# A hybrid encoder block on one core: one pool for value stage and pairs, sums on VectorE, weights loaded earlier, values of two heads computed in the attention stage

## The chip, the cores and the metric

The kernel runs on one core of a Trainium2 chip. A core has a matrix engine (TensorE, PE in the profile, with its weight loads as PEld), VectorE (DVE), ScalarE (ACT), GpSimd (POOL) and SyncE (SP), which issues DMAs. Compute engines read and write tiles in the on-chip memory; matmuls write into eight banks of accumulators. The metric is the device time of one execution in microseconds; the median of several runs is compared.

## The reference, cut to what matters

```
h  = rmsnorm(x) * (1 + scale) + shift               # scale, shift, gate from silu(c) @ w_ada
q, k, v, z_gla, ra_f, ra_b, u, vs, z_gmlp, m_gla, m_gmlp = split(h @ w_in)
# branch 1: 4 heads of gated linear attention in both directions, chunks of 64 tokens;
# decays from ra_f, ra_b; q, k of 128 columns a head, v of 256 columns a head
o     = rmsnorm(o_forward + o_backward) * gla_norm_g
y_gla = (o * silu(z_gla)) @ w_br_gla
# branch 2: spatial gating in chunks of 128 tokens
sg     = einsum(gmlp_ws, layernorm(gelu(vs))) + gmlp_bs
y_gmlp = (gelu(u) * sg * silu(z_gmlp)) @ w_br_gmlp
out = rmsnorm(x + gate * ((sigmoid(m_gla) * y_gla + sigmoid(m_gmlp) * y_gmlp) @ w_out)) * final_g
```

All is 1024 tokens by 1024 columns in float32.

## The kernel before, in words

Every large matmul works on operands split in two: a rounded part ("hi", cast on ScalarE) and the rest ("lo", subtracted on VectorE); `split_w` makes both, and three matmuls (hi·hi, hi·lo, lo·hi) stand for one product over 128 rows. The stages, in program order:

1. **Norm and vs, first half.** `h` (the activation `H`, 16 tiles of two chunks by 512 tokens, hi and lo) is made while the first half of vs is computed.
2. **Layer norm and spatial mixing** (`vs1`, `ln`, `spatial`). The power of the norm runs on GpSimd. The mixed rows `sg` go to DRAM.
3. **Value stage.** `dense_v23` (heads 2 and 3, 512 columns at once), `dense_v0` (head 0 with the 32 gate logits `ra`, 288 columns) and `dense_v1` (head 1). Each token tile's values are split by `v_out` and stored to DRAM on SP's queue. Beside it `sums` makes sums and differences of four quarters of H (the tiles `TS`, t0 to t3): four additions and four subtractions per call on GpSimd (L459 to L468), then four splits.
4. **Pairs** (`pair`, 16 of them). Two blocks of 128 output columns are computed together from the sums (a scheme that needs seven products instead of eight). Two raw weight tiles `wa`, `wb`, their sums `wsum` (four half-size additions on GpSimd, L574 to L581), and four splits per pair. The evaluation gives u, z_gmlp and the two merge gates, which go to DRAM. Half of the second-half H is stored away in `b12_d` and loaded again afterwards.
5. **Attention stage.** For each head, dense projections (q, k, two of z for the next head; for the last head, the eight blocks `dense_yb` of the other branch) are traced first, and then, at a higher priority, four units of the gated linear attention: `front` (decays, scan, scores) and `body` (states and outputs). Values come back from DRAM with `load_v` on GpSimd's queue.
6. **Last projections.** `ya` (eight blocks), then the output projection `dense_o` in two halves, the norm and the stores.

The order of instructions on each engine comes from a planner: it walks the program by priority (trace order, `high_priority` moves a block forward) and by the times of its own model, and fixes one order per engine; semaphores are added by it. `issue_after` puts a block's instructions behind a named one on the same engine. Tiles come from pools: all tiles of one tag share its `bufs` slots, and a new tile waits until an old one of its tag is no longer read. A pool that is closed gives its space to pools opened later; a tile there waits for the old tiles in its space.

The tags that the steps touch: `h` (30 slots of 4 KB: H, the sums, value weights, and in the attention stage q, k, z and the loaded values), `x` and `ws` in the pool X of the first stages, the pool M1 (spatial mixing and the copies of the values), the pool W (pairs; each kind of tile with its own slots), `wp` and F (weights and work tiles of the attention stage). The accumulators are `pd` (three banks), `pm`, `po` (two each) and `pk` (one).

Of the kernel before, what the change touches and what calls it, by code (L numbers as in the profile page):

```python
# [9 lines left out]
F32 = mybir.dt.float32  # L10
# [7 lines left out]
P = 128  # L18
# [26 lines left out]
def hybrid_block_kernel(ctx: ExitStack, tc: tile.TileContext, x, wf, wt, wada, wgate, wvr, wst, alpha, abias,  # L45
# [13 lines left out]
    def close(cm):  # L59
        cm.__exit__(None, None, None)  # L60
# [114 lines left out]
    def dense_fm(b, x, evac):  # L175

        hi, lo = fm_weights(b)
        for half in range(2):
            acc = pd()
            for k in range(KC):  # L180
                TE.matmul(acc, lhsT=hi[:, k, :], rhs=x.hi(k, half), start=(k == 0), stop=False)  # L181
                TE.matmul(acc, lhsT=hi[:, k, :], rhs=x.lo(k, half), start=False, stop=False)  # L182
                TE.matmul(acc, lhsT=lo[:, k, :], rhs=x.hi(k, half), start=False, stop=(k == KC - 1))  # L183
            evac(half, acc)
# [207 lines left out]
    for t in range(6, 8):  # L392
        evac_vs(0)(t, accs[t])
    close(cS)

# [55 lines left out]
    spatial(0)  # L451


    TS = [Act(f"t{i}") for i in range(4)]

    def sums(c, ins):
        def whole(cc_, half):
            r = xt([P, 2, 512], F32, "r")
            G.tensor_tensor(out=r, in0=H.h[cc_][half].bitcast(F32), in1=H.l[cc_][half].bitcast(F32), op=ALU.add)  # L459
# [8 lines left out]
        G.tensor_tensor(out=r21, in0=r21, in1=r22, op=ALU.subtract)  # L468
        with tc.issue_after(ins.ins):
            for i, r in ((1, r22), (2, r12), (0, r11), (3, r21)):  # L470
                hi, lo = TS[i].make(c, 0)
                split_w(flat(r), flat(hi), flat(lo))


    def v_out(h, n, t, acc):

        vh = Mp.tile([P, n * HV], F32R, tag="vh", bufs=3, name=nm("vh"))
        vl = Mp.tile([P, n * HV], F32R, tag="vl", bufs=3, name=nm("vl"))
        ins = S.copy(vh, acc)
        V.tensor_tensor(out=vl, in0=acc, in1=vh.bitcast(F32), op=ALU.subtract)  # L480
        for i in range(n):
            for d, v in zip(v_d, (vh, vl)):
                nc.sync.dma_start(d[h + i, t // 4, :, (t % 4) * HV:(t % 4 + 1) * HV],
                                  v[:, i * HV:(i + 1) * HV].bitcast(F32))
        return ins
# [10 lines left out]
    def dense_v0():  # L496
        pieces = []
        for a, e in ((0, 3), (3, 6), (6, 8)):
            n = (e - a) * NV0
            w = wpool[0].tile([P, 1024], F32, tag="ws", bufs=2, name=nm("ws"))  # L500
            nc.sync.dma_start(w[:, 0:n], wvr[:, a * NV0:e * NV0])
            hi, lo = ht([P, e - a, NV0], F32R, "tvh"), ht([P, e - a, NV0], F32R, "tvl")
            split_w(w[:, 0:n], flat(hi), flat(lo))
            for k in range(a, e):
                pieces.append((hi[:, k - a, :], lo[:, k - a, :]))
        for t in TOKENS:
            acc = pd()[:, 0:NV0]
            v_steps(acc, pieces, t)
            S.copy(ra[:, t, :], acc[:, HV:NV0])
            ins = v_out(0, 1, t, acc[:, 0:HV])  # L510
        return ins

    def dense_v1():
        pieces = []
        for j in range(2):
            w = stage(wt[WV1 + j])
            hi, lo = xt([P, 4, HV], F32R, "tvh"), xt([P, 4, HV], F32R, "tvl")
            split_w(w, flat(hi), flat(lo))
            for k in range(4):
                pieces.append((hi[:, k, :], lo[:, k, :]))  # L520
        for t in TOKENS:
            acc = pd()[:, 0:HV]
            v_steps(acc, pieces, t)
            ins = v_out(1, 1, t, acc)
        return ins

    def dense_v23():
        ws = tm_weights(WV23, ht)
        pieces = [(ws[k // 2][0][:, k % 2, :], ws[k // 2][1][:, k % 2, :]) for k in range(KC)]
        for t in TOKENS:  # L530
            acc = pd()
            v_steps(acc, pieces, t)
            ins = v_out(2, 2, t, acc)
        return ins
# [25 lines left out]
    def wt_(tag, n):  # L560
        return [Wp.tile([P, n], F32R, tag=tag + x, bufs=1, name=nm(tag + x)) for x in "hl"]

    def tmp(name):
        return Wp.tile([P, 512], F32, tag=name, bufs=2, name=nm(name))

    def pair(ba, bb, evac):

        wa = Wp.tile([P, 1024], F32, tag="wa", bufs=2, name=nm("wa"))
        wb = Wp.tile([P, 1024], F32, tag="wb", bufs=2, name=nm("wb"))
        nc.sync.dma_start(wa, wf[ba])  # L570
        nc.sync.dma_start(wb, wf[bb])
        L, R = slice(0, 512), slice(512, 1024)
        ws = Wp.tile([P, 1024], F32, tag="wsum", bufs=1, name=nm("wsum"))
        G.tensor_tensor(out=ws[:, L], in0=wb[:, L], in1=wb[:, R], op=ALU.add)  # L574
# [35 lines left out]
    def pair_m(b0, d, i):  # L610

        def ev(b, half, acc):
            m = Wp.tile([P, 512], F32, tag="z", bufs=4, name=nm("m"))
            S.activation(m, acc, AF.Tanh, scale=0.5)
            G.dma_start(d[2 * i + b, :, half * 512:half * 512 + 512], m)
        pair(b0 + 2 * i, b0 + 2 * i + 1, ev)

    def pair_uz(i):
# [5 lines left out]
        def ev_z(b, half, acc):  # L624
            sl = slice(half * 512, half * 512 + 512)
            sg = Wp.tile([P, 512], F32, tag="sg", bufs=3, name=nm("sgl"))
            G.dma_start(sg, sg_d[2 * i + b, :, sl])
            z = Wp.tile([P, 512], F32, tag="z", bufs=4, name=nm("z"))
            S.activation(z, acc, AF.Tanh, scale=0.5)
# [61 lines left out]
    for i in range(1, 4):  # L691
        pair_m(FB_MA, ta_d, i)
    close(cW)

# [9 lines left out]

    def dense_q(h):
        q_t[h] = vt([P, T], F32, "q")

        def ev(half, acc):
            S.activation(q_t[h][:, half * 512:half * 512 + 512], acc, AF.Copy, scale=float(P) ** -0.5)  # L709
        dense_fm(FB_Q + h, H, ev)  # L710

    def dense_k(h):
        k_t[h] = vt([P, T], F32, "k")

        def ev(half, acc):
            S.copy(k_t[h][:, half * 512:half * 512 + 512], acc)
        dense_fm(FB_K + h, H, ev)

    def dense_z(h):
        for j in range(2):  # L720
# [7 lines left out]
            dense_fm(FB_Z + h * 2 + j, H, ev)  # L728

    cw, wp = pool("wp")  # L730
    wpool[0] = wp
# [6 lines left out]

    r3 = Fp.tile([P, NT, 3, 32], F32, name="r3")
    for t in range(NT):  # L740
# [21 lines left out]
    low_rank(0)  # L762
    dense_q(0)
    dense_k(0)
    smask = Fp.tile([P, 512], F32, name="smask")
# [188 lines left out]
    def dense_yb(j):  # L954
# [44 lines left out]
    cY, Yp = pool("Y", side="right")  # L999
    M_hi, M_lo = [], []  # L1000
    for j in range(KC):
        if j < 6:
# [8 lines left out]
        def ev_ya(half, acc):  # L1011
# [60 lines left out]

    def dense_o(pieces, evac, tokens):
        for t in tokens:
            acc = pd()
            tsl = slice(t * P, t * P + P)
            for k in range(KC):
                tm_step(acc, pieces, M_hi[k][:, tsl], M_lo[k][:, tsl], k)
            evac(t, acc)
# [38 lines left out]
def _layout(inputs):  # L1118
# [48 lines left out]
```

## Time and profile before

| | |
|---|---|
| runs | 1156.87, 1157.23, 1160.45 us; median 1157.23 |
| profiled execution | 1160.66 us, span 1159.0 us |
| TensorE clock granted, mean | 0.97 |
| busy: PE, DVE, ACT, POOL | 1080.1, 650.9, 463.7, 279.8 us |
| moved by DMA | 143.89 MB |

In the profile, the span is the time from the first to the last instruction. A row of matmuls names the accumulator and its operands (`pd<-hh,wh`); `Lnnn` is a line of the kernel file. "Idle before" a group is the time in which its engine did nothing before it, with what released it. Matmuls overlap, so that their durations (400 ns for 512 columns) are longer than their distance.

### The profile page before, as it was taken

The page shows a single profiled execution, that of the slowest core. Times are in us where ns is not written, and L with a number is a line of the kernel's source. Part 1 is how long each engine was busy: PE and PEld are TensorE (multiplying, and loading weights), DVE is VectorE, ACT ScalarE, POOL GpSimd, SP SyncE. Part 2 cuts the span into 40 slices and gives each one's busy share as a digit, 9 for nine tenths or more (in the row PEclk, how much of TensorE's full clock was granted, in tenths as well). Part 3 has the DMA queues.
Part 4 walks back from the last instruction along what each step waited for, and adds up shares of the span by engine and source line. Part 5 has one row for each costly group of instructions (what it writes and reads, how often), then busy time and mean ns, then how long its engine had stood idle before and what let it go on. Part 6 is the DMA issues. An engine that isn't in the chain of part 4 may idle for free.

```text
span 1159.0 us, 13934 instructions
## 1 busy us (share of the span) xinstructions
PE 1080.1 (93%) x5204; PEld 901.4 (78%) x5204; DVE 650.9 (56%) x1033; ACT 463.7 (40%) x772; POOL 279.8 (24%) x278
## 2 busy tenths in 40 slices
PE   6899995979999999999799997996989999999997
PEld 4777884977888888888578886885868887888876
DVE  6855435434464646465534668677688656555232
ACT  5353212223333333335244657665665423222132
POOL 3211444406343434434200001002011010012420
PEclk9899998999999999999989998998999999999999
DMA  8542242342333333223931112113244337513312
GB/s 328 199 163 88 71 155 82 111 135 102 128 118 110 111 107 120 98 100 117 364 117 55 37 37 74 72 37 127 74 159 160 109 116 266 208 52 127 149 73 109
DMA packets 53142, 143.89 MB, mean 124 GB/s; under 512 B 6895, under 2 KB 15087, under 8 KB 53074
## 3 DMA queue, kind: packets, MB, share of 16 engines
q1 hardware_dynamic: 40898, 102.42, 25.5%
q0 software_dynamic: 12176, 40.58, 9.5%
q8 instruction: 41, 0.67, 0.2%
q14 instruction: 27, 0.22, 0.1%
HBM read 104.18 MB, written 38.80 MB: 123 GB/s over the span
## 4 chain that ended last, share of the span: by engine, by line
PE 79%; DVE 7%; issue 4%; DMA 4%; ACT 4%; POOL 1%; SPq 0%; POOLq 0%; DVEq 0%; ACTq 0%
PE pd L182 10%; PE pd L181 10%; PE pd L183 10%; PE pd L200 4%; PE pd L201 4%; PE pd L199 4%; PE po L552 3%; PE po L550 3%; PE po L551 3%; PE pd L490 2%; PE pd L491 2%; PE pd L492 2%; PE pd L552 2%; PE pd L551 2%; PE pd L550 2%
## 5 line engine op out<-in xcount | busy, mean ns | idle before, releaser
L181 PE MATMUL pd<-hh,wh 128*128 128x512 f32 x256 | 102.3, 400 | 2.3 <-ACT q L709 2.3
L182 PE MATMUL pd<-hl,wh 128*128 128x512 f32 x256 | 101.9, 398 | 0.0
L183 PE MATMUL pd<-hh,wl 128*128 128x512 f32 x256 | 101.1, 396 | 0.0
L210 POOL TENSOR_TENSOR r<-ms,nhalf 128x1 f32<-128x1 f32 (+1 forms) x24 | 21.4, 893 | 306.7 <-DVE ms L209 306.6
L181 PEld LDWEIGHTS pd<-hh,wh 128*128 128x128 f32 x256 | 49.0, 192 | 12.2 <-ACT q L709 2.8
L550 PE MATMUL pd<-hh,ah 128*128 128x512 f32 x128 | 50.7, 396 | 8.3 <-ACT ah L162 8.3
L162 ACT CAST wh<-ws 128x1024 fp32r<-128x1024 f32 x32 | 33.6, 1049 | 61.8 <-PE pd L182 60.4
L183 PEld LDWEIGHTS pd<-hh,wl 128*128 128x128 f32 x256 | 48.9, 191 | 9.7
L182 PEld LDWEIGHTS pd<-hl,wh 128*128 128x128 f32 x256 | 49.0, 191 | 9.1
L182 PE MATMUL pd<-gl,wh 128*128 128x512 f32 x128 | 50.6, 396 | 2.1 <-DVE gl L163 2.1
L182 PE MATMUL pd<-ggl,wh 128*128 128x512 f32 x128 | 50.6, 397 | 2.0 <-DVE ggl L163 2.0
L181 PE MATMUL pd<-ggh,wh 128*128 128x512 f32 x128 | 50.8, 400 | 1.4 <-ACT ggh L162 1.4
L552 PE MATMUL pd<-hh,al 128*128 128x512 f32 x128 | 50.4, 394 | 0.0
L551 PE MATMUL pd<-hl,ah 128*128 128x512 f32 x128 | 50.4, 394 | 0.0
L181 PE MATMUL pd<-gh,wh 128*128 128x512 f32 x128 | 50.3, 395 | 0.0
L183 PE MATMUL pd<-gh,wl 128*128 128x512 f32 x128 | 50.3, 394 | 0.0
L183 PE MATMUL pd<-ggh,wl 128*128 128x512 f32 x128 | 49.9, 393 | 0.0
L199 PE MATMUL pd<-th,mh 128*128 128x512 f32 x120 | 46.2, 400 | 2.5 <-ACT th L162 2.5
L163 DVE TENSOR_TENSOR wl<-ws,wh 128x1024 fp32r<-128x1024 f32 x32 | 39.1, 1221 | 16.5 <-ACT wh L162 16.4
L200 PE MATMUL pd<-tl,mh 128*128 128x512 f32 x120 | 47.8, 398 | 0.1
L201 PE MATMUL pd<-th,ml 128*128 128x512 f32 x120 | 47.0, 392 | 0.0
L163 DVE TENSOR_TENSOR al<-wa,ah 128x1024 fp32r<-128x1024 f32 x16 | 19.6, 1225 | 46.7 <-ACT ah L162 46.7
(322 smaller groups left out, 3118.7 us busy)
## 6 DMA issues: line engine op xcount, KB each, us to landing
ws<-in_wf SPq DMA_DIRECT2D x32, 512.0 KB, 3.5
ws<-in_wt SPq DMA_DIRECT2D x22, 512.0 KB, 3.9
wa<-in_wada SPq DMA_DIRECT2D x16, 512.0 KB, 5.1
wa<-in_wf SPq DMA_DIRECT2D x16, 512.0 KB, 4.0
wb<-in_wf SPq DMA_DIRECT2D x16, 512.0 KB, 3.5
xn<-in_x SPq DMA_DIRECT2D x8, 512.0 KB, 6.0
sg_d<-sg POOLq DMA_DIRECT2D x16, 256.0 KB, 2.4
vh_d<-vh SPq DMA_DIRECT2D x32, 128.0 KB, 1.8
```

What stands on the lines that cost most here:

```text
L162: S.copy(hi, w)
L163: V.tensor_tensor(out=lo, in0=w, in1=hi.bitcast(F32), op=ALU.subtract)
L181: TE.matmul(acc, lhsT=hi[:, k, :], rhs=x.hi(k, half), start=(k == 0), stop=False)
L182: TE.matmul(acc, lhsT=hi[:, k, :], rhs=x.lo(k, half), start=False, stop=False)
L183: TE.matmul(acc, lhsT=lo[:, k, :], rhs=x.hi(k, half), start=False, stop=(k == KC - 1))
L199: TE.matmul(acc, lhsT=xh, rhs=hi[:, k % 2, :], start=(k == 0), stop=False)
L200: TE.matmul(acc, lhsT=xh, rhs=lo[:, k % 2, :], start=False, stop=False)
L201: return TE.matmul(acc, lhsT=xl, rhs=hi[:, k % 2, :], start=False, stop=(k == KC - 1))
L490: TE.matmul(acc, lhsT=H.hi_t(k, t), rhs=hi, start=(k == 0), stop=False)
L550: TE.matmul(acc, lhsT=a, rhs=xh(k), start=(first and k == 0), stop=False, skip_group_check=not first)
L551: TE.matmul(acc, lhsT=a, rhs=xl(k), start=False, stop=False, skip_group_check=not first)
L552: TE.matmul(acc, lhsT=b, rhs=xh(k), start=False, stop=(k == 3), skip_group_check=not first)
```

## The change

- **One pool.** M1 and X are closed before the value stage, and W is opened there. In W there are two tags only: `w4` (11 slots of 4 KB) and `w2` (15 slots of 2 KB), which the value stage, the sums and the pairs share.
- **Sums on VectorE.** All additions and subtractions of `sums` go from GpSimd to VectorE, and each result is split as soon as it is there. The first call comes after head 0's values and is no longer held behind a copy.
- **Head 0's value weights ahead.** They are loaded and split at the end of stage 1.
- **Heads 2 and 3.** `dense_v23` is gone; `dense_v` takes one head at a time, head 1 in the value stage, heads 2 and 3 as the first dense work beside heads 0 and 1 in the attention stage.
- **q and k of head 0** are computed before W closes, with weights in its slots; the copies `r3` of the gate logits go to tag `h`.
- **Last projections.** The first two `ya` weights are loaded first, and three accumulators take their first six steps ahead; their three matmuls come in the order hi·hi, lo·hi, hi·lo. The first `dense_o` takes seven of eight steps for three token tiles ahead.

```diff
-    def fm_weights(b):
-        w = stage(wf[b])
-        hi = wpool[0].tile([P, KC, P], F32R, tag="wh", bufs=2, name=nm("wh"))
-        lo = wpool[0].tile([P, KC, P], F32R, tag="wl", bufs=2, name=nm("wl"))
+    def fm_weights(b, new=None):
+        if new is None:
...
+        else:
+            w = new([P, 1024], F32, "ws")
+            nc.sync.dma_start(w, wf[b])
+            hi, lo = new([P, KC, P], F32R, "wh"), new([P, KC, P], F32R, "wl")
         split_w(w, flat(hi), flat(lo))
         return hi, lo
...
     for t in range(6, 8):
         evac_vs(0)(t, accs[t])
+    v0_w = []
+    for a, e in ((0, 3), (3, 6), (6, 8)):
+        n = (e - a) * NV0
+        w = wpool[0].tile([P, 1024], F32, tag="ws", bufs=2, name=nm("ws"))
+        nc.sync.dma_start(w[:, 0:n], wvr[:, a * NV0:e * NV0])
+        hi, lo = ht([P, e - a, NV0], F32R, "tvh"), ht([P, e - a, NV0], F32R, "tvl")
+        split_w(w[:, 0:n], flat(hi), flat(lo))
...
     spatial(0)
+    close(cM)
+    close(cX)
+    cW, Wp = pool("W")
+    def w4(shape, dtype, name):
+        return Wp.tile(shape, dtype, tag="w4", bufs=11, name=nm(name))
+    def w2(shape, dtype, name):
+        return Wp.tile(shape, dtype, tag="w2", bufs=15, name=nm(name))
...
-    def sums(c, ins):
+    def sums(c, ins=None):
         def whole(cc_, half):
-            r = xt([P, 2, 512], F32, "r")
-            G.tensor_tensor(out=r, in0=H.h[cc_][half].bitcast(F32), in1=H.l[cc_][half].bitcast(F32), op=ALU.add)
+            r = w4([P, 2, 512], F32, "r")
+            V.tensor_tensor(out=r, in0=H.h[cc_][half].bitcast(F32), in1=H.l[cc_][half].bitcast(F32), op=ALU.add)
             return r
...
-        G.tensor_tensor(out=r11, in0=r12, in1=r11, op=ALU.subtract)
+        V.tensor_tensor(out=r11, in0=r12, in1=r11, op=ALU.subtract)
         r22 = whole(c + 2, 1)
-        G.tensor_tensor(out=r12, in0=r22, in1=r12, op=ALU.subtract)
-        G.tensor_tensor(out=r22, in0=r22, in1=r11, op=ALU.subtract)
+        V.tensor_tensor(out=r12, in0=r22, in1=r12, op=ALU.subtract)
+        cast(2, r12)
+        V.tensor_tensor(out=r22, in0=r22, in1=r11, op=ALU.subtract)
+        cast(0, r11)
         r21 = whole(c + 2, 0)
...
-    sums(0, dense_v23())
     v_last = dense_v0()
-    dense_v1()
+    sums(0)
+    dense_v(1, w4, w4, w2)
     sums(1, v_last)
-    close(cM)
-    close(cX)
-    cW, Wp = pool("W")
...
-        wa = Wp.tile([P, 1024], F32, tag="wa", bufs=2, name=nm("wa"))
-        wb = Wp.tile([P, 1024], F32, tag="wb", bufs=2, name=nm("wb"))
+        wa, wb = w4([P, 1024], F32, "wa"), w4([P, 1024], F32, "wb")
...
     for i in range(1, 4):
         pair_m(FB_MA, ta_d, i)
-    close(cW)
...
+    dense_q(0, w4)
+    dense_k(0, w4)
+    close(cW)
     cw, wp = pool("wp")
...
-    r3 = Fp.tile([P, NT, 3, 32], F32, name="r3")
+    r3 = ht([P, NT, 3, 32], F32, "r3")
...
     for h in range(HEADS):
+        if h + 2 < HEADS:
+            dense_v(h + 2, ws_new, ht, vo_new)
         if h + 1 < HEADS:
...
+    ya_w[0], ya_w[1] = fm_weights(FB_YA), fm_weights(FB_YA + 1)
+    AHEAD = ((0, 0), (0, 1), (1, 0))
+    for j, half in AHEAD:
+        ya_steps(j, half, 0, 6)
...
-        dense_fm(FB_YA + j, GO, ev_ya)
+        if j >= 2:
+            ya_w[j] = fm_weights(FB_YA + j)
+        for half in range(2):
+            ya_steps(j, half, 6 if (j, half) in AHEAD else 0, KC)
+            ev_ya(half, ya_acc[j, half])
...
-    def dense_o(pieces, evac, tokens):
+    def dense_o(pieces, evac, tokens, ahead=()):
...
+        for t in ahead:
+            o_steps(t, 0, KC - 1)
         for t in tokens:
-            acc = pd()
...
+            o_steps(t, KC - 1 if t in ahead else 0, KC)
+            evac(t, accs[t])
...
-    dense_o(w_o[0], ev_first, range(NT))
+    dense_o(w_o[0], ev_first, range(NT), range(3))
```

`dense_v(h, raw, new, out)` is `dense_v1` with the head and the places of its tiles as arguments: two raw weight tiles from `raw`, their splits from `new`, the copies from `out` (`ws_new`: the two staged weights of `wp`; `vo_new`: four slots of their own).

More of the change, by code (lines that the diff above doesn't have):

```diff
@@ L393, in hybrid_block_kernel @@
         evac_vs(0)(t, accs[t])
+    v0_w = []
[5 more added lines that the diff above has]
+        split_w(w[:, 0:n], flat(hi), flat(lo))
+        for k in range(a, e):
+            v0_w.append((hi[:, k - a, :], lo[:, k - a, :]))
     close(cS)
@@ L467, in sums @@
+        cast(0, r11)
         r21 = whole(c + 2, 0)
[L468 to L478, printed above, removed]
+        V.tensor_tensor(out=r21, in0=r21, in1=r22, op=ALU.subtract)
@@ L479, in v_out @@
+        cast(1, r22)
+        cast(3, r21)
+    def v_out(h, t, acc, new):
+        vh, vl = new([P, HV], F32R, "vh"), new([P, HV], F32R, "vl")
         ins = S.copy(vh, acc)
         V.tensor_tensor(out=vl, in0=acc, in1=vh.bitcast(F32), op=ALU.subtract)
[L481 to L484, printed above, removed]
+        for d, v in zip(v_d, (vh, vl)):
+            nc.sync.dma_start(d[h, t // 4, :, (t % 4) * HV:(t % 4 + 1) * HV], v.bitcast(F32))
@@ L496, in dense_v0, with dense_v @@
     def dense_v0():
[L497 to L505, printed above, removed]
         for t in TOKENS:
             acc = pd()[:, 0:NV0]
-            v_steps(acc, pieces, t)
+            v_steps(acc, v0_w, t)
             S.copy(ra[:, t, :], acc[:, HV:NV0])
-            ins = v_out(0, 1, t, acc[:, 0:HV])
+            ins = v_out(0, t, acc[:, 0:HV], w2)
         return ins
-    def dense_v1():
+    def dense_v(h, raw, new, out):
         pieces = []
         for j in range(2):
-            w = stage(wt[WV1 + j])
-            hi, lo = xt([P, 4, HV], F32R, "tvh"), xt([P, 4, HV], F32R, "tvl")
+            w = raw([P, 1024], F32, "ws")
+            nc.sync.dma_start(w, wt[WV + 2 * (h - 1) + j])
+            hi, lo = new([P, 4, HV], F32R, "tvh"), new([P, 4, HV], F32R, "tvl")
             split_w(w, flat(hi), flat(lo))
@@ L523, in dense_v1 @@
             v_steps(acc, pieces, t)
[L524 to L530, printed above, removed]
-            acc = pd()
-            v_steps(acc, pieces, t)
-            ins = v_out(2, 2, t, acc)
-        return ins
-    sums(0, dense_v23())
+            v_out(h, t, acc, out)
     v_last = dense_v0()
-    dense_v1()
+    sums(0)
+    dense_v(1, w4, w4, w2)
     sums(1, v_last)
-    close(cM)
-    close(cX)
-    cW, Wp = pool("W")
     def prod(acc, wh, wl, xh, xl, first):
@@ L612, in ev @@
         def ev(b, half, acc):
-            m = Wp.tile([P, 512], F32, tag="z", bufs=4, name=nm("m"))
+            m = w2([P, 512], F32, "m")
             S.activation(m, acc, AF.Tanh, scale=0.5)
@@ L962, in dense_yb, with ws_new, vo_new @@
         dense_fm(FB_YB + j, GG, ev)
+    def ws_new(shape, dtype, name):
+        return wp.tile(shape, dtype, tag="ws", bufs=2, name=nm(name))
+    def vo_new(shape, dtype, name):
+        return Gp.tile(shape, dtype, tag="vo", bufs=4, name=nm(name))
     for h in range(HEADS):
+        if h + 2 < HEADS:
+            dense_v(h + 2, ws_new, ht, vo_new)
         if h + 1 < HEADS:
@@ L1000, in hybrid_block_kernel, with ya_steps @@
     M_hi, M_lo = [], []
+    ya_w, ya_acc = {}, {}
+    def ya_steps(j, half, k0, k1):
+        if k0 == 0:
+            ya_acc[j, half] = pd()
+        acc = ya_acc[j, half]
+        hi, lo = ya_w[j]
+        for k in range(k0, k1):
+            TE.matmul(acc, lhsT=hi[:, k, :], rhs=GO.hi(k, half), start=(k == 0), stop=False)
+            TE.matmul(acc, lhsT=lo[:, k, :], rhs=GO.hi(k, half), start=False, stop=False)
+            TE.matmul(acc, lhsT=hi[:, k, :], rhs=GO.lo(k, half), start=False, stop=(k == KC - 1))
+    ya_w[0], ya_w[1] = fm_weights(FB_YA), fm_weights(FB_YA + 1)
+    AHEAD = ((0, 0), (0, 1), (1, 0))
+    for j, half in AHEAD:
+        ya_steps(j, half, 0, 6)
     for j in range(KC):
```

54 lines of the change are left out of this document (32 added, 22 removed).

## The prediction

> **What bounds the kernel now.** I read the page first (engines, slices, chain), then the list of what TensorE waited for, then windows cut around each of its gaps, and last the short timelines of VectorE and GpSimd in them.
>
> ```profile
> span 1159.0 us, 13934 instructions
> ## 1 busy us (share of the span) xinstructions
> PE 1080.1 (93%) x5204; PEld 901.4 (78%) x5204; DVE 650.9 (56%) x1033; ACT 463.7 (40%) x772; POOL 279.8 (24%) x278
> ...
> PEclk9899998999999999999989998998999999999999
> ...
> PE 79%; DVE 7%; issue 4%; DMA 4%; ACT 4%; POOL 1%; SPq 0%; POOLq 0%; DVEq 0%; ACTq 0%
> ```
>
> TensorE is the bound: 93% busy, 79% of the chain that ends last. The change removes no matmul work, so all it can win is the 79 us in which PE is idle and the dips of the granted clock after them. Who ended those gaps:
>
> ```profile
> PE po L747 <- DVE r L741: 9.0, 1, 9.0
> PE pd L550 <- ACT ah L162: 8.3, 1, 8.3
> PE pd L491 <- DVE tvl L163: 7.4, 1, 7.4
> PE pk L831 <- DVE s L850: 7.1, 5, 2.7
> PE pd L490 <- ACT tvh L162: 5.3, 1, 5.3
> ...
> PE pd L182 <- DVE gl L163: 2.1, 1, 2.1
> ```
>
> Columns: total, times, longest. Five of the six are single waits at stage borders: L490/L491 (values of heads 2, 3 to those of head 0), L550 (values to the first pair), L747 (last pair to the attention stage), L182 (attention stage to the last projections). L831 is the state chain inside the attention stage. Windows around them, in us: length, busy time of each engine (instructions), granted TensorE clock, DMA share, GB/s:
>
> ```profile
> core 0: us, PE busy (x) PEld busy (x) DVE busy (x) ACT busy (x) POOL busy (x), PEclk, DMA share, GB/s
> 189.60:195.00 5.40, 0.14 (x1) 0.14 (x1) 4.50 (x4) 5.37 (x7) 2.44 (x1) 0.98 0.29 97
> 195.00:208.00 13.00, 5.59 (x22) 5.25 (x23) 12.62 (x5) 1.30 (x2) 12.92 (x5) 0.50 0.12 31
> 215.00:218.00 3.00, 1.68 (x13) 1.64 (x13) 1.98 (x4) 0.46 (x2) 0.00 (x0) 1.00 0.37 123
> 234.00:254.00 20.00, 20.00 (x179) 20.00 (x178) 7.61 (x11) 5.46 (x11) 0.69 (x2) 1.00 0.31 104
> 254.30:262.00 7.70, 0.03 (x1) 0.00 (x0) 0.67 (x3) 0.94 (x3) 0.67 (x2) 0.85 0.87 300
> 262.00:267.00 5.00, 4.32 (x10) 3.03 (x11) 1.23 (x1) 1.23 (x2) 3.88 (x3) 0.55 0.41 169
> 270.00:570.00 300.00, 299.86 (x1319) 247.24 (x1318) 170.82 (x200) 106.60 (x146) 124.05 (x131) 1.00 0.36 125
> 572.30:581.30 9.00, 0.00 (x0) 0.00 (x0) 2.30 (x8) 1.67 (x2) 2.72 (x5) 0.77 1.03 417
> 581.30:587.00 5.70, 5.67 (x18) 4.73 (x19) 4.72 (x9) 2.11 (x3) 0.00 (x0) 0.50 0.75 274
> 590.00:700.00 110.00, 110.00 (x549) 93.04 (x548) 60.72 (x107) 62.65 (x108) 0.00 (x0) 1.00 0.12 39
> 705.00:735.00 30.00, 22.37 (x121) 18.44 (x120) 23.74 (x50) 20.51 (x44) 5.57 (x9) 0.83 0.33 119
> 790.00:815.00 25.00, 16.04 (x70) 12.32 (x69) 17.41 (x40) 15.89 (x34) 5.06 (x7) 0.80 0.31 106
> 845.00:865.00 20.00, 15.30 (x71) 11.95 (x70) 19.17 (x38) 16.27 (x27) 2.73 (x2) 0.91 0.55 184
> 970.00:972.50 2.50, 0.38 (x2) 0.19 (x2) 2.50 (x4) 1.48 (x3) 0.00 (x0) 1.00 0.87 265
> 972.50:977.00 4.50, 4.50 (x13) 3.51 (x13) 2.10 (x3) 0.84 (x1) 0.00 (x0) 0.62 0.97 310
> 1044.00:1100.00 56.00, 56.00 (x247) 46.09 (x246) 20.90 (x30) 11.57 (x22) 20.59 (x13) 1.00 0.37 137
> ```
>
> A gap's price is its idle time plus busy time x (1 - clock). A (values to values): 5.26 + 7.41 + 5.59 x 0.50 + 1.32 = 16.8 us. B (values to pairs): 7.67 + 0.68 + 4.32 x 0.45 = 10.3. C (pairs to attention): 9.0 + 5.67 x 0.50 = 11.9. D (head borders in the attention stage): 7.63 + 22.37 x 0.17 = 11.4 for heads 0/1, 8.96 + 16.04 x 0.20 = 12.2 for 1/2, 4.70 + 15.30 x 0.09 = 6.1 for 2/3, together 29.7. E (entry to the last projections): 2.12 + 4.50 x 0.38 = 3.8. All five: 72.5 us.
>
> **The change part by part.** *Values of two heads moved.* Before, heads 2 and 3 take 192 matmuls of 512 columns; after, 384 of 256. The pitch at 512 is 300/1319 = 0.227 us, at 256 20/177 = 0.113 us, so 43.6 us against 43.4: no price, only another place. The weight loads run at 20.00 of 20 us at 256 columns and do not stretch the pitch.
>
> *Gap A.* It exists because head 0's weights (tvh, tvl) are split only when the sums are done and the values of heads 2, 3 have freed their tiles. Loaded ahead, their three splits fall in the layer-norm stage. This border becomes layer-norm to head 0's values, and A goes: -16.8. What is late next: the value copies now lie in the new pool, whose space partly overlaps tiles that the spatial mixing still reads. Head 0's 192 matmuls of 288 columns (an estimate from 0.113: 24 us) have three accumulators, 9 us, before a copy must land. From no stall to those copies waiting some 8 us (gap B's length, the nearest pool border). I take 2, since freed token tiles are there for the first copies. In its favour, the last layer-norm's power on GpSimd no longer queues behind the sums.
>
> *Gap B and the sums.* The pairs' weights no longer wait for a pool to close: they come during head 1's values. -10.3. But VectorE now does 8 additions per call of sums, two calls, next to 4 splits each. Prices:
>
> ```profile
> 191.19 1.22 DVE L163 TENSOR_TENSOR t1l<-r,t1h 128x1024 fp32r<-128x1024 f32 x1 [0.25 <-ACT t1h L162]
> 192.34 1.22 DVE L163 TENSOR_TENSOR t2l<-r,t2h 128x1024 fp32r<-128x1024 f32 x1
> 193.47 3.44 DVE L163 TENSOR_TENSOR t0l<-r,t0h 128x1024 fp32r<-128x1024 f32 x1
> ```
> ```profile
> 192.56 9.82 POOL L459 TENSOR_TENSOR r<-hh,hl 128x1024 f32<-128x1024 f32 x3 [12.98 <-DVE t1l L163]
> ```
> ```profile
> 226.72 0.42 DVE L480 TENSOR_TENSOR vl<-pd,vh 128x256 fp32r<-128x256 f32 x1 [2.76 <-ACT vh L479]
> ```
>
> The same subtraction takes 1.22 us alone and 3.44 once GpSimd adds two tiles beside it. One call of sums is 12 x 1.22 = 14.6 us. Beside head 1's values (192 x 0.113 = 21.7 us of PE) VectorE has 14.6 + 8 x 0.42 + 3 x 1.22 + 0.7 for the first pair's splits = 22.4 us: 0.7 us too much. The first pair's two products on H alone (24 x 0.227 = 5.5 us) give slack. Its four half-size GpSimd additions may each push one VectorE operation from 1.22 to 3.44, 8.9 us. So 0 to 9 us of stall; I take 3, nearer the uncontended rows, since one call can run early beside head 0's values.
>
> The Trainium skill ("SBUF — State Buffer", "SBUF: two separate sides") says the port pair VectorE and GpSimd share is an exclusive lock, the later one blocking until the first is done. That speaks against moving sums to VectorE while GpSimd prepares weights, and by it I would take the upper end, 9; the row of 3.44 agrees with it, and I keep 3 only because few GpSimd operations stand there.
>
> *Gap C.* Its chain is a copy of the gate logits that waited for the pairs' last stores:
>
> ```profile
> DVE r L741 <- DMA ta_d<-m: 5.9, 1, 5.9
> ```
>
> After, that copy has a tile outside the closing pool, and q and k of head 0 (2 x 48 x 0.227 = 21.8 us of PE) run from weights in the old pool. Both first halves need no reloaded H. They cover C, its DMA burst (417 GB/s) included: -11.9. If z's first weights must wait for the space of k's, a load and its splits come back as in gap B (7.7 us idle): 0 to 9, I take 1.
>
> *The attention stage.* From 590 to 700 dense work fills PE to 110.00 of 110; the head borders starve, because PE then waits for the state chain alone (L831). The change puts 21.7 us more dense work into each of heads 0 and 1. It also adds 16 copies and subtractions, four splits (16 x 0.42 + 4 x 1.22 = 11.6 us of VectorE), 32 stores and 4 loads on SP, all beside full PE; VectorE is 60.72 of 110 busy there. A store on SP waits for its token's copy with the next weight load behind it; two staged weights cover one token's 2.7 us. What limits the gain is the pool of 30 tiles:
>
> ```profile
> ACT q L709 <- DMA g_d<-zg: 2.0, 1, 2.0
> ```
>
> The next head's q had to wait for a tile that the previous head's output store freed. After, H (16), values (4), two heads of q, k, z (8) and the value weights (4) ask for 32 of 30, so head 3's value weights get their four tiles only as head 0 ends. Ends: -29.7 (all borders filled) to +11.6 (new VectorE work all on the state chain). I take half of border 0/1 (5.5), most of 1/2 (7.5: 21.7 us of new work against 12.2 lost, and by then the tiles come in turn) and nothing of 2/3: -13.
>
> *Last projections, started ahead.* Three accumulators with 18 matmuls each (12 us) go before the wait for the last head's z. One of the three reads the second half's tiles, which are made late. From -3.8 to +1.5 (reordering), taken -2. The Trainium skill ("TensorE: Matmul & The Clock Gate", Part 1) lets the clock drop only after an idle window of about 3.4 us; gap E, idle 2.1 us, shows 0.62 behind it. By the page E would be worth 2.1, by the row 3.8; the row decides.
>
> *Output projection ahead.* PE is busy 56.00 of 56 us across that border: 0 (-1 to +2).
>
> Sum: -16.8 + 2 - 10.3 + 3 - 11.9 + 1 - 13 - 2 = -48.0. The profiled execution took 1160.66 us, 3.4 over the median of 1157.23; 48 off the median gives **1109**.
>
> **The rivals.** *1. Slower: shared slots stall the pairs.* Now 16 pairs run 299.86 of 300 us because raw, split and summed weights have buffers of their own. After, 11 shared tiles hold nine per pair and two prefetched. If a prefetch takes the tile that a split needs, each of 15 changes of pair waits for GpSimd and two splits, an estimated half of gap B's 7.7 us: 15 x 4 = +60, time near 1169. It decides from 48/15 = 3.2 us a pair. Against: the early raw tiles are free when the next pair's splits need them. 6%.
>
> *2. The borders stay.* Tiles and the state chain limit the heads, D gains nothing: 1122. For: the tile count. 22%.
>
> *3. The value stage becomes VectorE-bound* by the contention above: the sums end 9 us late and PE restarts at half clock, 2 more: 11 for the 3 taken, 1117; with a little lost elsewhere 1117 to 1126. For: the 3.44 row. 14%.
>
> *4. All filled:* D gives 25 to 29, A to C no new stall: 1088 to 1100. For: 110.00 of 110 where dense work stands. 17%.
>
> *5. The gaps only move:* the new pool waits where the old borders did, a clear gain of 0 to 17 us: 1140 to 1158. For: its space is that of the pools it replaces. 8%.
>
> **How the numbers follow.** The forecast, 1100 to 1117, has 33%. The range 1089 to 1135 holds it with rivals 2, 3 and nearly all of 4: about 83%, a little less for the unknown stalls. 0.3% (3.5 us) is about what a measurement of this kernel tells from no change. Faster: all but rival 1 and the last part of rival 5, 0.91; same 0.03; slower 0.06.
>
> **What would show it.** Right: no PE wait on tvh, tvl, on the first pair's ah, or on the copy of L741; q and k between last pair and attention; PE idle near 43 us instead of 79 (A 14.0, B 8.4, C 9.0, D some 9, E 1 gone, 6 new); the clock row without the digits 8 at those borders. Wrong: a PE wait on t1h or t1l at the first pair; on vh at head 0's values; single PE waits at each pair; in the attention stage, borders as wide as now or longer waits on L850's successor; PE idle at z's first weights.

## The result, and the profile after

| | before | after |
|---|---|---|
| median | 1158.84 us (1156.87 to 1161.45) | 1127.17 us (1125.17 to 1130.17) |
| ratio | | 0.9728, 95% interval 0.9694 to 0.9761 |
| profiled execution, span | 1160.66 us, 1159.0 us | 1125.17 us, 1123.5 us |

The change makes the kernel 31.7 us faster by the medians and 35.5 us by the profiled spans. The forecast was 1109 us with a range of 1089 to 1135: the time lies in the range but outside the forecast's own span of 1100 to 1117, and the gain is two thirds of the 48 us that were predicted. The page of the kernel after:

```profile
span 1123.5 us, 14279 instructions
...
PE 1070.5 (95%) x5396; PEld 903.4 (80%) x5396; DVE 665.0 (59%) x1057; ACT 461.9 (41%) x780; POOL 229.1 (20%) x262
...
PEclk9899989999999999999899999999999999999999
```

TensorE is idle for 53 us (1123.5 less 1070.5) instead of 79, and the digits 8 at the head borders are gone. Whom TensorE waited for (total, times, longest):

```profile
PE pd L520 <- DVE vl L512: 9.0, 2, 7.6
PE pk L558 <- DVE u L614: 6.5, 10, 1.2
PE pd L186 <- ACT wh L162: 5.5, 1, 5.5
...
PE pd L186 <- ACT ggh L162: 2.7, 1, 2.7
...
PE pk L838 <- DVE s L857: 0.4, 1, 0.4
```

The waits on tvl, tvh, the first pair's ah and the copy of the gate logits have all disappeared, and the state chain of the attention stage (L857, before L850) fell from 7.1 us to 0.4. Three new ones stand in their place: vl at head 0's values, u in the pairs' accumulator `pk` (TensorE waits until VectorE has read it), and wh at the first z projection. The windows of the kernel after, cut around them:

```profile
core 0: us, PE busy (x) PEld busy (x) DVE busy (x) ACT busy (x) POOL busy (x), PEclk, DMA share, GB/s
150.00:154.00 4.00, 3.15 (x28) 2.96 (x26) 1.50 (x2) 0.00 (x0) 1.43 (x3) 1.00 0.47 180
154.00:162.00 8.00, 0.43 (x4) 0.24 (x3) 6.62 (x9) 1.96 (x5) 1.08 (x2) 0.70 0.83 287
162.00:168.00 6.00, 6.00 (x27) 6.00 (x28) 6.00 (x8) 3.05 (x5) 0.00 (x0) 0.54 0.20 68
172.00:182.00 10.00, 8.44 (x62) 7.97 (x61) 10.00 (x13) 2.10 (x5) 0.14 (x1) 1.00 0.57 183
182.00:195.00 13.00, 12.89 (x107) 12.69 (x106) 12.70 (x12) 7.54 (x12) 6.85 (x4) 1.00 0.27 92
200.00:530.00 330.00, 323.47 (x1433) 264.38 (x1432) 182.88 (x205) 108.78 (x152) 118.80 (x130) 1.00 0.35 125
545.00:552.20 7.20, 0.66 (x3) 0.25 (x2) 2.77 (x6) 6.29 (x9) 0.53 (x1) 0.83 0.23 76
552.20:558.00 5.80, 5.80 (x17) 4.57 (x18) 5.14 (x9) 3.59 (x5) 0.00 (x0) 0.62 0.45 155
590.00:810.00 220.00, 219.88 (x1315) 195.07 (x1315) 152.53 (x297) 135.01 (x263) 14.14 (x22) 1.00 0.26 90
810.00:830.00 20.00, 16.29 (x79) 13.36 (x78) 17.93 (x34) 15.11 (x27) 1.07 (x1) 0.91 0.48 159
934.00:944.00 10.00, 7.07 (x29) 4.89 (x29) 5.91 (x6) 4.77 (x6) 0.55 (x1) 1.00 0.84 278
```

Priced as in the prediction (idle time plus busy time x (1 - clock)), the balance of the two profiled executions is this:

| place | before | after | gain | forecast |
|---|---|---|---|---|
| A, start of head 0's values | 16.8 | 0.85 + 7.57 + 0.13 + 2.76 + 1.56 = 12.9 | 3.9 | 14.8 |
| B, values to first pair | 10.3 | 0.1 | 10.2 | 7.3 |
| the pairs (16 of them) | 0.1 | 6.5 | -6.4 | 0 |
| C, entry to the attention stage | 11.9 | 6.54 + 0.11 + 2.20 = 8.9 | 3.0 | 10.9 |
| D, head borders | 29.7 | 0.12 + 3.71 + 1.47 = 5.3 | 24.4 | 13 |
| E, entry to the last projections | 3.8 | 2.9 | 0.9 | 2 |

These give 36.0 us. Two small places remain. The second half of vs (80 to 100 us of the span) loses 1.7 us less, where GpSimd was busy for 3.66 us beside VectorE's splits and now is for 0.56 (rows below, before and then after; no run tried that place alone). A new 0.75 us lies between 580 and 590 us. With both the sum is 36.9 us against 35.5 between the spans.

```profile
80.00:100.00 20.00, 17.97 (x75) 13.43 (x74) 14.02 (x24) 7.98 (x11) 3.66 (x2) 1.00 0.53 187
```
```profile
80.00:100.00 20.00, 19.64 (x83) 15.16 (x82) 10.58 (x22) 8.07 (x11) 0.56 (x1) 1.00 0.39 136
```

### The profile page after: what moved, and what is told of

Its sections match the earlier page's. It is cut to its first block, busy times and chain, and to the rows that moved or that the text cites. A ratio compares the mean times of both kernels' runs of the same rounds, so it can differ in the third digit from the quotient of the medians.

```text
span 1123.5 us, 14279 instructions
## 1 busy us (share of the span) xinstructions
PE 1070.5 (95%) x5396; PEld 903.4 (80%) x5396; DVE 665.0 (59%) x1057; ACT 461.9 (41%) x780; POOL 229.1 (20%) x262
## 4 chain that ended last, share of the span: by engine, by line
PE 69%; DVE 5%; DMA 4%; ACT 3%; issue 2%; POOL 0%; SPq 0%; POOLq 0%; DVEq 0%; ACTq 0%
PE pd L186 7%; PE pd L187 7%; PE pd L188 7%; PE po L560 3%; PE po L558 3%; PE po L559 3%; PE pd L1024 2%; PE pd L1025 2%; PE pd L1026 2%; PE pd L205 2%; PE pd L206 2%; PE pk L558 2%; PE pd L204 2%; PE pd L560 2%; PE pk L560 2%; PE pk L559 2%
## 5 line engine op out<-in xcount | busy, mean ns | idle before, releaser
L520 PE MATMUL pd<-tvh,hh 128*128 128x256 f32 (+1 forms) x256 | 75.0, 293 | 9.2 <-DVE vl L512 9.0
L522 PE MATMUL pd<-tvh,hl 128*128 128x256 f32 (+1 forms) x256 | 74.4, 291 | 0.0
L521 PE MATMUL pd<-tvl,hh 128*128 128x256 f32 (+1 forms) x256 | 74.3, 290 | 0.0
L186 PEld LDWEIGHTS pd<-hh,wh 128*128 128x128 f32 x256 | 48.8, 190 | 15.2 <-ACT wh L162 5.8
L520 PEld LDWEIGHTS pd<-tvh,hh 128*128 128x128 f32 x256 | 49.8, 195 | 10.3 <-DVE vl L512 10.1
L521 PEld LDWEIGHTS pd<-tvl,hh 128*128 128x128 f32 x256 | 49.9, 195 | 0.2
L522 PEld LDWEIGHTS pd<-tvh,hl 128*128 128x128 f32 x256 | 49.8, 195 | 0.0
```

The lines of the kernel that those rows point to most:

```text
L520: TE.matmul(acc, lhsT=H.hi_t(k, t), rhs=hi, start=(k == 0), stop=False)
L521: TE.matmul(acc, lhsT=H.hi_t(k, t), rhs=lo, start=False, stop=False)
L522: TE.matmul(acc, lhsT=H.lo_t(k, t), rhs=hi, start=False, stop=(k == KC - 1))
```

## The experiments

Each ratio is against the kernel before, run on the same chip; the medians of two runs can come from different chips. "After" has 0.9728 (0.9694 to 0.9761).

### Gap A: the copies' space

The timelines of the kernel after at the end of the spatial mixing (start, length, engine, operation, in brackets the idle time before and its releaser), ScalarE first, then VectorE:

```profile
156.91 0.37 ACT L511 CAST vh<-pd 128x256 fp32r<-128x256 f32 x1 [7.18 <-DVE sg L447]
```
```profile
156.80 4.62 DVE L484 TENSOR_TENSOR r<-hh,hl 128x1024 f32<-128x1024 f32 x4
161.34 0.41 DVE L512 TENSOR_TENSOR vl<-pd,vh 128x256 fp32r<-128x256 f32 x1
```

ScalarE holds the first value copy for 7.18 us, until VectorE has made the last `sg` of the spatial mixing: the copy's slot lies in space of the closed pools. Which tile of the mixing was there is not shown. It was not the row `sg` itself, since its store to DRAM is issued only at 157.17 us, after the copy has begun. VectorE then does four additions of the sums before the first `vl`, and only this frees an accumulator. The run e1_copies_h gives the copies of head 0 tiles of the tag `h` instead, which lie in no closed pool:

```diff
-            ins = v_out(0, t, acc[:, 0:HV], w2)
+            ins = v_out(0, t, acc[:, 0:HV], ht)
```

> The copies of head 0's values take slots of the 30-tile tag instead of the new pool's small slots, whose space the spatial mixing still uses. Theory (the copies wait for that space): the PE wait on the value subtraction at head 0's values, 7.6 us, and the half clock behind it, 2.8, go; the profile's span falls by 7 to 11 us against the changed kernel's 1123.5. Rival (VectorE is late, its four additions of the first sums, 4.6 us, stand ahead of the subtraction): most of the wait stays, span falls by 0 to 4.

It took 1118.34 us, ratio 0.9636 (0.9612 to 0.966). Its windows:

```profile
154.00:162.00 8.00, 8.00 (x64) 8.00 (x63) 5.91 (x7) 1.03 (x5) 1.08 (x2) 1.00 0.60 181
182.00:195.00 13.00, 11.08 (x79) 9.93 (x78) 13.00 (x12) 8.10 (x11) 10.04 (x4) 0.95 0.42 142
195.00:200.00 5.00, 5.00 (x19) 4.00 (x18) 4.51 (x5) 2.26 (x3) 0.31 (x2) 0.79 0.51 169
```

TensorE is busy 8.00 of 8 us where it had 0.43. So A's stall comes from the space of the copies: 8.8 us by the medians, 11.6 by the spans. The four additions are still there, 4.62 us from 157.94 us on, but five `vl` now come before them, and TensorE loses nothing by them. The other two rows show what A had hidden: now VectorE is full (13.00 of 13 us) as the first pair starts, and 1.92 + 0.55 + 1.05 = 3.5 us are lost there. That is the 3 us that the prediction took for B. The runs e5, e6 and e8 to e13 below all contain this edit; "with the copies in `h`" names this kernel.

### The sums: VectorE or GpSimd

With the copies in `h`, the additions and subtractions of `sums` go back to GpSimd (run e5_sums_gpsimd):

```diff
-            V.tensor_tensor(out=r, in0=H.h[cc_][half].bitcast(F32), in1=H.l[cc_][half].bitcast(F32), op=ALU.add)
+            G.tensor_tensor(out=r, in0=H.h[cc_][half].bitcast(F32), in1=H.l[cc_][half].bitcast(F32), op=ALU.add)
...
```

> Head 0's copies in the 30-tile tag (as in e1_copies_h, span 1111.9), and the additions and subtractions of the sums back on GpSimd. Theory (the sums belong on VectorE, since on GpSimd 16 operations of 2.4 to 3.4 us outlast the 47 us of values left there): the first pair waits for its sums, span 1115 to 1130. Rival (VectorE full before the first pair, 13.0 of 13 us in e1, is the dearer place): the small waits at the first pair go, span falls by 2 to 5.

It took 1137.03 us, ratio 0.9813 (0.9786 to 0.9841), 18.7 us more than with the sums on VectorE. The first pair waited for the splits of its weight sum (4.8 us for sh, 2.3 for sl), since GpSimd was still at the sums. And the wait on vl was back with 5.8 us, though the copies had their space. The view by lines names what stood before that `vl` on VectorE:

```profile
L667 DVE SCALAR_TENSOR_TENSOR gsc<-gth,pcol 128x8 f32<-128x8 f32 x1 | 13.8, 13793 | 0.0
```

This small operation with two operands in on-chip memory takes 0.15 us in the kernel after. Here it takes 13.79, from 160.01 us on, while GpSimd does six operations of the sums from 159.76 to 173.78 us without a pause. So VectorE, though full, is the better place for the sums.

### The head borders

The values of heads 2 and 3 are put back into the value stage, on the kernel after (run e3_values_back):

```diff
+    dense_v(2, w4, w4, w2)
+    dense_v(3, w4, w4, w2)
...
-        if h + 2 < HEADS:
-            dense_v(h + 2, ws_new, ht, vo_new)
```

> The values of heads 2 and 3 are computed in the value stage again, behind head 1's, one head at a time; all else is as in the changed kernel. Theory (moved dense work fills the head borders, 24 us): the borders 0/1 and 1/2 are back, PE idle and low clock of 18 to 25 us in the attention stage, span 1140 to 1150. Rival (the borders were filled by q and k of head 0 being done earlier and the other changes): span within 5 us of 1123.5.

It took 1150.03 us, ratio 0.9916 (0.9893 to 0.9939): 22.9 us of the gain are gone. The three borders are back, in its windows:

```profile
690.00:735.00 45.00, 37.36 (x189) 31.06 (x188) 34.78 (x71) 31.59 (x61) 6.60 (x10) 0.89 0.28 94
780.00:810.00 30.00, 23.41 (x107) 19.28 (x107) 22.41 (x47) 21.13 (x42) 4.49 (x7) 0.83 0.31 102
825.00:855.00 30.00, 26.62 (x117) 21.34 (x116) 26.08 (x48) 21.00 (x36) 3.29 (x3) 0.83 0.48 163
```

They cost 11.7 + 10.6 + 7.9 = 30.2 us, as before (29.7), and the waits on the state chain (4.7 us in `pk`) are back with them. The moved values are the whole of D.

### Entry to the attention stage

After the last pair, q and k of head 0 run as forecast, and then z waits 5.5 us for its first weight. ScalarE in the kernel after:

```profile
550.52 0.63 ACT L785 ACTIVATE e<-e 128x512 f32<-128x512 f32 x1
551.06 1.98 ACT L162 CAST wh<-ws 128x1024 fp32r<-128x1024 f32 x2
```

The cast of that weight comes behind the start of the first attention unit (L785). Its raw weight was there in time (the load was issued at 532.73 us, and such loads took at most 5.0 us to land). Is the cast late by its place on the engine, or by the space of the split weight? Three runs:

1. Run e4_z_ahead: the first block of z is also computed before W is closed, on the kernel after (`dense_z(0, (0,), w4)` ahead of `close(cW)`).

> The first z block of head 0 is also computed before the pairs' pool closes, with weights in its slots, 10.9 us more cover. Theory (the remaining 8.9 us at the border to the attention stage are z's first weights, whose cast stands on ScalarE behind the first unit's chain): the wait of 5.5 us on that cast and the half clock go, span falls by 5 to 9 us. Rival (the wait moves to the second z block, whose weights come just as late): span falls by less than 2.

It took 1128.06 us, 0.9725 (0.9708 to 0.9741): nothing gained. The wait went to the next weight (3.6 us) and to the operands of the last projections. The rival stands.

2. Run e9_z_weights_first: with the copies in `h`, z's first weights get a priority above the attention unit's:

```diff
+    with tc.high_priority(offset=2 * PRI):
+        z_first = fm_weights(FB_Z)
     with tc.high_priority(offset=PRI):
         front(0, 0)
```

> As e1_copies_h, and the cast and subtraction of the first z weights of head 0 get priority over the first attention unit. Theory (at that border PE waits because ScalarE does the unit's chain with two table loads first): the 5.5 us wait on the cast shrinks below 2 and the clock stays up, span falls by 4 to 8 us to 1104 to 1108. Rival (the weights wait for their space until k's last matmul and for their load, not for ScalarE's order): the wait stays at 4 us and more, span falls by less than 2.

It took 1117.85 us, 0.9654 (0.9628 to 0.9681), against 0.9636 without it, and the wait was still 5.5 us. Its ScalarE shows why this decides less than it seems: the cast stands behind the unit's start as before.

```profile
538.45 0.63 ACT L785 ACTIVATE e<-e 128x512 f32<-128x512 f32 x1
538.99 1.98 ACT L162 CAST wh<-ws 128x1024 fp32r<-128x1024 f32 x2
```

A higher priority did not move the cast; what an earlier place alone would bring is not tested.

3. Run e10_z_weights_h: as 2, with z's first weights, raw and split, in the tag `h`: `z_first = fm_weights(FB_Z, ht)`.

> As e9_z_weights_first, but the first z weights of head 0 (raw and split) take slots of the 30-tile tag, not of the pool that opens in the space of the pairs' pool. Theory (in e9 priority changed nothing since that space came free too late, so that the planner gave ScalarE the unit's chain first): the 5.5 us wait on the cast is gone, the clock stays up, span 1103 to 1108. Rival (the load comes late or the unit's chain itself holds PE): the wait stays under another name, span within 3 of e1's 1111.9.

It took 1108.87 us, 0.9563 (0.9534 to 0.9591), and TensorE has no gap at this border:

```profile
530.00:545.00 15.00, 15.00 (x72) 12.49 (x71) 5.31 (x9) 8.70 (x11) 1.04 (x2) 1.00 0.12 39
545.00:565.00 20.00, 20.00 (x130) 18.23 (x130) 16.08 (x27) 14.85 (x24) 0.00 (x0) 1.00 0.48 155
```

With this space the same cast runs at 526.91 us, while k is still being computed. So the cause is the space, which is all that differs from 2. By the program, a tile in a pool that takes over W's bytes must wait for W's last readers, and those are the matmuls of k, which end near 544 us in the kernel after. That its cast came only at 551.06, behind the unit's start, is read as the planner's choice under this limit and not tested by itself. Between 2 and 3 lie 9.0 us by the medians and 13.2 by the profiled spans.

### Starting ahead

With the copies in `h`, nothing is started ahead (run e6_no_ahead): `AHEAD = ()`, and the first `dense_o` without its fourth argument.

> As e1_copies_h, but nothing of the last two projections is started ahead; the first two ya weights are still loaded first. Theory (started ahead they gain 1 us or less, both borders cost about what they did): span 1110 to 1114; idle at the border into ya 2 to 3 us, none into the output projection. Rival (they hide 2 us and more): span 1114 to 1118 with a longer wait for the last head's z.

It took 1118.02 us, 0.964 (0.9613 to 0.9668), against 0.9636 with it. From 930 to 1110 us TensorE is busy 171.81 us without and 171.96 us with it. The two edits gain nothing that these runs can tell.

### The pairs

Ten waits for the evacuation of `pk` (the VectorE operation that reads the accumulator, L614) cost 6.5 us, five of them 0.33 us and five 0.6 to 1.2. The prediction's rival 1 would blame the shared slots. With the copies in `h`, each kind of tile of a pair gets slots of its own again (run e8_own_tags):

> As e1_copies_h, but in the pool each kind of pair tile has slots of its own again, as before the change (the value stage and q, k of head 0 borrow them). Theory (the shared slots changed the order of the seven products, and the waits of 6 us in the pairs come from it): PE is full again in the pairs, span 1104 to 1108, unless a border costs what the pairs gain. Rival (the waits come from VectorE and GpSimd getting in each other's way in the pairs whatever the slots): idle in the pairs stays at 5 to 7 us, span within 3 of 1111.9.

It took 1130.42 us, 0.9751 (0.9727 to 0.9775): slower than with the shared slots, and the waits stayed, 14 of them with 7.9 us. Slots of their own do not remove the waits. Next the accumulator (run e2_two_z): on the kernel after, `Z = pm()` (two banks) in place of `Z = pk_()` (one).

> The pairs' accumulator Z takes a tag with two banks instead of the single one. Theory (in the new order the next pair's first product on Z stands closer behind the last one's than its VectorE sum can free the bank): the ten PE waits of 6.5 us in the pairs go, span falls by 5 to 8 us. Rival (the waits show that VectorE itself is late, held by GpSimd): the waits reappear under another accumulator, span falls by less than 2.

It took 1180.21 us, 1.0179 (1.0158 to 1.02). Its total says little, since the gate's matmul shares `pm` and stood 43.0 us there for its weights. But the pairs can be read: the waits on `pk` are gone, others came (9.8 us for ScalarE's copy p of `pd`), and from 200 to 460 us TensorE is busy 254.69 us against 255.69 in the kernel after. So a second bank removes these waits, and TensorE's idle time only goes elsewhere.

What differs is the order. TensorE before, and then after, at a change of pair:

```profile
305.58 0.39 PE L552 MATMUL pk<-hh,fl 128*128 128x512 f32 x1
305.80 0.39 PE L552 MATMUL pd<-hh,al 128*128 128x512 f32 x1
...
308.75 0.39 PE L550 MATMUL pk<-t0h,sh 128*128 128x512 f32 x1
```
```profile
308.86 0.39 PE L560 MATMUL pk<-hh,fl 128*128 128x512 f32 x1
...
310.03 0.50 PE L558 MATMUL pk<-t0h,sh 128*128 128x512 f32 x1 [0.33 <-DVE u L614]
```

Here, before, 12 matmuls in `po` and one in `pd` lie between the last use of `pk` by one pair and the first by the next, 3.17 us. After, the planner puts only two matmuls there, and the evacuation takes longer than that. Over all 15 changes of pair: before, 13, 18 or 24 matmuls lie between, 18 at twelve of them, and none waits. After, 24 lie there at five changes, and none waits; two at six changes and eight at four, and these are the ten waits.

The trace of the kernel after tells the ten apart. At the five waits of 0.33 us two matmuls lie between, and VectorE had been idle for 2.03 us before the evacuation: it was not late, the distance is too short. At the four changes with eight matmuls (0.63 to 1.20 us, 3.9 in all) the evacuation stands behind an operation of the `sg` gate that takes 3.03 to 3.04 us; the first of them:

```profile
286.63 3.03 DVE L640 SCALAR_TENSOR_TENSOR u<-u,z 128x512 f32<-128x512 f32 x1
289.59 0.68 DVE L614 TENSOR_TENSOR u<-pk,u 128x512 f32<-128x512 f32 x1
```

GpSimd makes two additions in that time, at 286.57 and 287.82 us. The tenth wait (1.02 us, two matmuls) stands behind another VectorE operation of 2.07 us.

The next run (e11_z_order, copies in `h`) lengthens the distance: it puts the first product in `pk` behind the third in `po`:

```diff
+        with tc.issue_after(t3.ins):
-        prod(Z, sh[:, L], sl[:, L], *T1, True)
+            prod(Z, sh[:, L], sl[:, L], *T1, True)
```

> As e1_copies_h, but in a pair the first product on accumulator Z is put behind the third product on Y, so that Z's single bank has three to four products of time (8 us and more) to be read. Theory (the planner's new order places it 1 to 4 us behind the last product on Z of the pair before, closer than VectorE's sum takes on the chip, and slots are not the cause): the waits on pk go, PE idle in 200 to 460 falls from 5 to below 1.5 us, span 1104 to 1108. Rival (VectorE and ScalarE are late in the pairs at all, as the waits on the copy p in e2 may mean): idle stays at 4 and more under another name.

It took 1136.07 us, 0.9809 (0.9786 to 0.9831). The waits on `pk` are gone, but `pd` now waits 18.0 us for ScalarE's copies, and 12.5 us of 260 are idle. Its VectorE shows why the chain is late:

```profile
277.21 2.99 DVE L642 SCALAR_TENSOR_TENSOR u<-u,z 128x512 f32<-128x512 f32 x1
280.13 0.68 DVE L616 TENSOR_TENSOR u<-pk,u 128x512 f32<-128x512 f32 x1
```

The same operation with two operands in on-chip memory takes 2.99 us while GpSimd makes two additions beside it (1.30 us from 277.13 us on, 1.26 from 278.39), the evacuation of `pk` follows it, ScalarE's copy follows that, and TensorE's `pd` last. The same edit on the kernel with z's weights in `h` (run e12_both):

> e10 and e11 together. If both theories hold, both waits are gone and span is 1096 to 1102; if one of them only moved a wait, 1103 to 1108.

It took 1127.17 us, 0.9729 (0.9707 to 0.975): worse again, by 18 us. Last, on the kernel with z's weights in `h`, the four half-size additions of a pair go to VectorE, so that little but DMA issues is left to GpSimd in the pairs (run e13_adds_vector):

```diff
-        G.tensor_tensor(out=ws[:, L], in0=wb[:, L], in1=wb[:, R], op=ALU.add)
+        V.tensor_tensor(out=ws[:, L], in0=wb[:, L], in1=wb[:, R], op=ALU.add)
...
```

> As the kernel with z's first weights in the 30-tile tag, but the four half-size additions of a pair's weights run on VectorE instead of GpSimd. Theory (a GpSimd addition holds up a VectorE operation with two inputs in on-chip memory, and through it the accumulator pk): the group of u<-u,z at the sg gate falls from a mean of 1273 ns to about 0.7 us, PE's 8 waits of together 4.3 us in pk for L614 go, and the idle time of PE from 200 to 460 us, 4.4 us, falls below 1.5; VectorE's busy time there rises from 153 by 16 x 4 additions of about 0.7 us less the contention, to some 175 to 185 of 260. Time 1103 to 1107 us. Rival (VectorE is late in itself, by the order of its work in the pairs): idle of 4 us or more stays, or grows, as VectorE has the additions ahead of the evacuations in its queue; time 1109 to 1116.

It took 1104.27 us, 0.9538 (0.9499 to 0.9577); the interval overlaps that of 0.9563, so no gain is shown. The group at the `sg` gate (busy time, mean ns) and the window of the pairs, for the kernel with z's weights in `h` and then for this one:

```profile
L640 DVE SCALAR_TENSOR_TENSOR u<-u,z 128x512 f32<-128x512 f32 x16 | 20.4, 1273 | 0.3
```
```profile
200.00:460.00 260.00, 255.58 (x1117) 208.56 (x1116) 153.04 (x171) 85.50 (x119) 103.32 (x109) 1.00 0.31 107
```
```profile
L640 DVE SCALAR_TENSOR_TENSOR u<-u,z 128x512 f32<-128x512 f32 x16 | 11.0, 688 | 0.3
```
```profile
200.00:460.00 260.00, 253.63 (x1108) 206.95 (x1107) 162.94 (x222) 85.43 (x118) 29.65 (x54) 1.00 0.31 105
```

The contention is real: without GpSimd's additions the operation falls from 1273 to 688 ns. But the idle time of TensorE rises from 4.4 to 6.4 us, all of it in nine waits on `pk`, so the theory's forecast fails and the rival's idle time stands. (The time lies where the theory put it, but it can't decide: the two profiled spans are 1101.9 and 1101.6 us.) Five of the nine are still 0.33 us, at changes with two matmuls between. VectorE at the longest of them:

```profile
450.71 0.69 DVE L581 TENSOR_TENSOR wsum<-wb 128x512 f32<-128x512 f32 x1 [3.91 <-DMA wb<-in_wf]
451.32 0.68 DVE L611 TENSOR_TENSOR p<-po,p 128x512 f32<-128x512 f32 x1
...
455.65 0.68 DVE L614 TENSOR_TENSOR u<-pk,u 128x512 f32<-128x512 f32 x1
```

An addition waits for a weight load that is late, and with it seven operations that stand between it and the evacuation L614 in VectorE's fixed order. The edit took one delay out of VectorE's work and put the additions in, so it shows that the move gains nothing, and not that the contention cost nothing. What is shown: the shared slots are not the cause, and with 8.4 us or more between (e11) no wait on `pk` is left. What is read from the traces: at all ten waits the planner left `pk` eight matmuls or fewer, and at four of them the contention made VectorE late on top. What stays open: no run put the order of the kernel before back into the one after, so the price of the order alone is not measured.

## Why the prediction was partly right

**The bound and the list of gaps: right.** TensorE's idle time and the clock behind it explain the difference (36.9 us priced, 35.5 between the spans). Forecast idle was near 43 us; it is 53. Three of the signs that the prediction named for being wrong came: waits at head 0's values, at changes of pair and at z's first weights.

**A: the replacement wait was mis-sized, 2 us taken, 12.9 measured.** The step named the right danger ("tiles that the spatial mixing still reads") and its upper end of 8, then chose 2 because freed token tiles would serve the first copies. They did not: the first copy waited for the last operation of the mixing. That copy then came behind four additions on VectorE, which the step did not count, and the clock fell to 0.54 behind the gap, also not counted.

**B: right, with its mechanism.** The gap is gone, and its price of 3 for a full VectorE shows as 3.5 once A is mended; in the kernel after, A's stall hid it. The named cause is there too: with the copies in `h`, four VectorE operations of 128x1024 at the first pair take 1.98 to 2.31 us beside GpSimd's additions where others take 1.21, together 4.0 us more (and not the 8.9 of the upper end). By the rule of the Trainium skill ("SBUF — State Buffer", "SBUF: two separate sides"), an exclusive lock, the prediction would have taken the upper end of 9. The traces agree with the lock itself, 1273 against 688 ns in the pairs and 13.79 us against 0.15 with the sums on GpSimd, but at the first pair it cost less.

**C: the same step failed as in A, 1 us taken, 8.9 measured.** That z's weights might have to wait for the space of k's was said, with 0 to 9 as its bounds; the low end was taken without a row for it. The run with the weights in `h` shows that the space was the cause, with the cast's place behind the attention unit as a part of the price.

**D: too small by half, 13 us taken, 24.4 measured.** The sum took half of border 0/1 and most of 1/2, since the pool of 30 tiles and the state chain would hold the rest. Neither did: from 590 to 810 us TensorE is busy 219.88 of 220. Only the border near 820 us, where it waits 2.73 us for ggh, remains; that is border 2/3, for which nothing was taken, and rightly (6.1 us before, 5.2 after). So 43.4 us of dense work (42.9 by the row, which has 179 matmuls and not 177) filled 24.4 us of gaps, and the caution about tiles (rival 2) had no ground that a run shows.

**E and the work started ahead: 2 us taken, 0.9 measured**, and without these edits the time is the same. **Output projection: nothing forecast, nothing there.**

**The pairs: no term in the sum, 6.4 us lost.** The prediction did not ask whether the planner would keep the order of the seven products. Rival 1 had the symptom, single waits at the changes of pair, with another cause and a tenth of its price.

In sum, the errors of A (10.9), C (7.9), the pairs (6.4) and E (1.1) cost 26.3 us of the forecast, and B (2.9), D (11.4) and the small places (0.9) gave 15.2 back. That the time still lies in the range is partly luck: the two largest errors, A and D, nearly cancel. A and C are one misjudgement: where the new tile's space is that of an old one, the sum took the wait as nearly hidden. Rival 5 (the new pool waits where the old borders did) had this mechanism, for these two of its places.

## What to carry to other kernels

When tiles or weights are moved ahead, ask whose bytes they take: at a border between pools, the time at which a tile comes free limits everything behind it, and a higher priority alone brought nothing here. Two such waits cost 8.8 and 9.0 us by the medians, and a tag that outlives the border removed both, to 1108.87 us, 0.9563 of the time before. Dense work put beside a dependent chain fills its gaps well: 43 us of it closed 24 us. And when the order on an engine is planned anew, look at single-bank accumulators: the distance between their last reader and their next writer can shrink unseen.

## What the runs showed of the hardware

The clock gate did not follow the length of the gap alone. In the kernel with z's weights in `h`, a wait of 2.09 us at the entry to the last projections left the clock at 1.00; in the kernel before, one of 2.12 us was followed by 0.72. The windows of the gap and of what follows, in this order:

```profile
918.10:920.60 2.50, 0.42 (x2) 0.00 (x1) 0.00 (x1) 1.04 (x1) 0.00 (x0) 1.00 1.01 366
920.60:923.00 2.40, 2.38 (x10) 1.99 (x11) 2.29 (x2) 1.85 (x2) 0.00 (x0) 1.00 1.05 398
```
```profile
969.80:972.30 2.50, 0.40 (x2) 0.00 (x0) 2.50 (x5) 1.68 (x3) 0.00 (x0) 1.00 0.87 267
972.30:974.00 1.70, 1.69 (x5) 1.33 (x6) 1.70 (x3) 0.00 (x0) 0.00 (x0) 0.72 0.95 246
```

The idle window of about 3.4 us in the Trainium skill ("TensorE: Matmul & The Clock Gate", Part 1) fits the first and not the second. What else decides was not tried.

The contention between VectorE and GpSimd showed its price in single operations with two operands in on-chip memory: 2.99 us for one of 0.69 us beside two additions, and 13.79 us for one of 0.15 us beside six that followed each other without a pause. So the VectorE operation did not get its turn between two GpSimd operations in these places, and its own size said little about the delay.
